# Spreading the weights' sums of an encoder block over mixer B, mixer A, the output branches and the output projection

## The chip, the cores and the metric

The kernel runs on one core of a Trainium2 chip. The core has five engines with a queue of their own each: TensorE (PE: matmuls and transposes), VectorE (DVE), ScalarE (ACT), GpSimd (POOL) and SyncE (SP). Each works off its queue in order. Here SP issues every DMA transfer. The metric is the device time of one execution in microseconds (us), lower is better.

## The reference, cut to what matters

One layer of a bidirectional encoder, for two sequences of 512 tokens with 1024 channels and shared weights, in float32:

```python
mod = silu(c) @ w_ada + b_ada                      # six vectors: sh1, sc1, gt1, sh2, sc2, gt2
h = rmsnorm(x, g_attn) * (1 + sc1) + sh1
z = h @ w_in                                       # mixer A, mixer B, two gates
oa = window_attention(...)                         # mixer A: 8 heads, 2 key heads, window of 128
ob = dense_attention(...)                          # mixer B: 8 heads, low-rank q and kv
mix = sigmoid(gla) * (oa @ w_o_a) + sigmoid(glb) * (ob @ w_o_b)    # the branches
x = x + gt1 * (mix @ w_out)                        # the output projection
h2 = rmsnorm(x, g_ffn) * (1 + sc2) + sh2
u = dwconv(h2 @ w_up, conv_w, conv_b)              # up-projection to 2 x 2816
ua, ug = split(u)
x = x + gt2 * ((silu(ug) * ua) @ w_down)
```

## The kernel before, in words

A product in float32 is made of three matmuls (`mm3`, L79): both operands are split into a high and a low part, and the product of the two low parts is left out. The splitting of weights is done by POOL (`split_pool`, L69) or by ACT and DVE (`split_fast`, L75).

The stages that matter here stand one after the other:

- **Mixers B and A** (L463 to L753). The rounds of one loop (L727) go over 64 units of mixer B and then 64 of mixer A. A unit is the scores of one head for 128 tokens. For each, PE makes scores (`scores`), DVE and ACT the softmax, POOL scales the rows by the inverse of their sum (L539), and PE transposes them (L545) three rounds later. Between, PE makes the matmuls of the two gates (`gates`, tile psg, L495); their results go out as gate_d.
- **Weights' sums** (`weight_sums`, L504). The up-projection below is computed from seven products of block sums in place of eight products of blocks (in the manner of Strassen and Winograd). Four of its weight operands are sums of four blocks of w_up. POOL makes them with four operations (L522 to L526) on a tile wsum that SP has loaded; SP then stores the tile to su_d in DRAM. There are 22 pieces c of w_up, each in two halves of 256 columns, so 44 tiles of 512 KB each, in two buffers. The generator is advanced by one step per round (L749), so one tile is done in three rounds. `keep_in_program_order` pins these instructions: POOL and SP keep the order in which they are written.
- **Branches** (L786 to L827). For each of 8 pieces f of 128 output channels, wo is loaded and split by POOL (`w_branch`), and for each sequence 24 matmuls follow (`branches`, tile psy); the gates come back as gt. At f = 4 the first half of w_out is loaded and split by POOL into the eight wt tiles (`w_half(0)`, L827).
- **Output projection** (L898 to L950). Two halves of 512 columns. `project_half` goes over two sequences and four blocks of tokens; each `project` is 24 matmuls (tile psx), a scaling and an addition on DVE, and a store to x1_d (L885). The second half's weights (`w_half(1)`, L949) take the same eight wt buffers, through seven raw buffers (wraw, L763), and are split by ACT and DVE.
- **Up-projection with convolution** (tiles px, py, pz, L980) and **down-projection** (psd). The first read of su_d is at 790.9 us.

PE's queue is fixed by the order in which the kernel is written, up to the choices of a scheduler; SP's and POOL's queues hold the pinned instructions in their written order, with the others between them.

Of the kernel before, what the change touches and what calls it, by code (L numbers as in the profile page):

```python
# [31 lines left out]
GW = 4 * AD + 2 * AD  # L32
FF = 2816
NP = FF // 128
EPS = 1e-6
BIG = -1e30

# [2 lines left out]
def encoder_block(ctx, tc, x, c_t, w_ada0, b_col, w_ada, b_ada, cols, w_z, w_g, gains, tabs, sink,  # L40
# [87 lines left out]
    with ExitStack() as st:  # L128
# [184 lines left out]
        with ExitStack() as s0:  # L313
# [140 lines left out]
            for _ in mods:  # L454
                pass

    mp = ctx.enter_context(tc.tile_pool(name="mp", bufs=1))

    def mblk(name, tag, shape=None, dt=F32R):
# [3 lines left out]
    with ExitStack() as st:  # L463
# [7 lines left out]
        def gates():  # L471
# [15 lines left out]
            for n in range(2 * KD):  # L487
                f, m = divmod(n, 2)
                for b in range(NB):
# [8 lines left out]
                    go = gw.tile([128, S], F32, name="go", bufs=2)  # L498
                    A.copy(go, ps)
                    SY.dma_start(gate_d[b, f, :, m], go)  # L500

        def weight_sums():  # L504

            pin = tc.keep_in_program_order
            halves = [(c, slice(256 * q, 256 * (q + 1))) for c in range(NP) for q in range(2)]
            ts = {}

            def load(n):  # L510
                if n < len(halves):
                    c, cs = halves[n]
                    ts[n] = gw.tile([128, 4, 256], F32, name="wsum", bufs=2)
                    pin(SY.dma_start(ts[n], w_up[c].rearrange("m q p n -> p (m q) n")[:, :, cs]))

            load(0)
            yield
            yield
            for n, (c, cs) in enumerate(halves):
                t = ts[n]  # L520
                load(n + 1)
                pin(G.tensor_add(t[:, 3], t[:, 2], t[:, 3]))  # L522
                pin(G.tensor_sub(t[:, 2], t[:, 0], t[:, 2]))
                yield
                pin(G.tensor_sub(t[:, 0], t[:, 3], t[:, 0]))
                pin(G.tensor_sub(t[:, 1], t[:, 1], t[:, 0]))  # L526
                yield
                pin(SY.dma_start(su_d[c, :, :, cs], t))
                yield

        def softmax(ps, n, plen):

# [179 lines left out]

        blocks = [PairB(b, g) for b in range(NB) for g in range(BH // 2)] + [GroupA(b, g) for b in range(NB) for g in range(AKV)]
        gate = gates()
        wsum = weight_sums()

        def fill(n):
            for _ in range(n):
# [8 lines left out]
        for n in range(len(todo) + LAG + 2):  # L727
            if n < len(todo):
                blk, u, first = todo[n]
                if first:  # L730
                    for _ in nxt:
                        pass
                    bi, since = blocks.index(blk), 0
                    nxt = blocks[bi + 1].prep() if bi + 1 < len(blocks) else iter(())
                scored.append((blk, u, blk.scores(u)))
            fill(5)
            for blk_, h in heads:
                blk_.values(h)
            heads = []
            if scored and (n >= LAG):  # L740
                blk_, u_, p_ = scored.pop(0)
                h = blk_.spread(u_, p_)
                if h is not None:
                    heads.append((blk_, h))
            if n < len(todo):
                if since >= blk.prep_from:
                    next(nxt, None)
                since += 1
            next(wsum, None)  # L749
        for _ in gate:  # L750
            pass
        for _ in wsum:
# [33 lines left out]
    with ExitStack() as s0:  # L786
        wk = s0.enter_context(tc.tile_pool(name="wko", bufs=2))
        ob = []
        raws = [mblk("o_raw0", "st", dt=F32), hblk("o_raw1", dt=F32)]
        for b in range(NB):  # L790
            SY.dma_start(raws[b], o_d[b].rearrange("q p n -> p q n"))
            o = [mblk(f"o{b}{q}", "st" if b else "pt") for q in range(2)]
            for q in range(8):
                split_fast(o[0][:, q, :], o[1][:, q, :], raws[b][:, q, :])
            ob.append(o)
        for b in range(NB):
            m_hi.append(hblk(f"m_hi{b}"))
            m_lo.append(hblk(f"m_lo{b}"))

        def w_branch(f):  # L800
            w = wk.tile([128, 2, 2, 4, 128], F32R, name="wo")
            for m in range(2):
                raw = wk.tile([128, 4, 128], F32, name="wo_raw", bufs=3)
                SY.dma_start(raw, w_o[f, :, m])
                split_pool(w[:, 0, m], w[:, 1, m], raw)
            return w

        def branches(f, b, w):
            gt = wk.tile([128, 2, S], F32, name="gt", bufs=2)
            SY.dma_start(gt, gate_d[b, f])  # L810
            A.activation(gt, gt, AF.Sigmoid)
            for m in range(2):
                ps = bank("psy")
                for k in range(4):
                    mm3(ps, w[:, 0, m, k, :], w[:, 1, m, k, :], ob[b][0][:, 4 * m + k, :], ob[b][1][:, 4 * m + k, :],
                        k == 0, k == 3)
                V.tensor_mul(gt[:, m, :], ps, gt[:, m, :])
            V.tensor_add(gt[:, 0, :], gt[:, 0, :], gt[:, 1, :])
            split_fast(m_hi[b][:, f, :], m_lo[b][:, f, :], gt[:, 0, :])

        for f in range(0, KD, 2):
            wo = [w_branch(f), w_branch(f + 1)]
            for b in range(NB):
                for q in range(2):
                    branches(f + q, b, wo[q])
            if f == 4:
                ws = w_half(0)  # L827

# [24 lines left out]
    with ExitStack() as s0:  # L853
# [91 lines left out]
            elif i == 2:  # L945
                first_sequence(0)

        project_half(0, (0, 1), lambda b, i: None)
        ws = w_half(1)  # L949
        project_half(1, (1, 0), operands)  # L950

# [217 lines left out]
```

## Time and profile before

| | |
|---|---|
| median of three runs | 1460.76 us (1458.72 to 1462.15) |
| profiled execution | 1463.69 us |
| its span in the trace | 1461.9 us |
| PE busy | 1395.4 us (95%) |
| DVE busy | 941.7 us (64%) |
| ACT busy | 679.5 us (46%) |
| POOL busy | 609.0 us (42%) |
| transfers | 255 MB, 175 GB/s on average |

A busy PE is not a PE at its peak: matmuls overlap, so a product of 512 columns is shown with 0.39 us where the next one starts 0.23 us later. What PE loses is read from the times at which it is not busy, from what ended them, and from the clock that was granted. In the trace, an idle time stands in brackets at the row of the instruction that came after it, with the instruction that released it.

### The profile page before, as it was taken

To read this page: it belongs to the slowest core of one execution; us is meant where nothing else is said; L and a number is where in the kernel's file an instruction comes from. 1 tells how busy PE (TensorE), PEld (TensorE's weight loads), DVE (VectorE), ACT (ScalarE), POOL (GpSimd) and SP (SyncE) were. 2 spreads that over 40 slices of the span, in tenths; PEclk is the share of its full clock that TensorE was granted. 3 is DMA by queue.
4 is the path that set the end of the run, shared out by engine and by line. 5 is a ranking of instruction groups with operands and counts; after the bars stand their busy time and mean duration, and the time that the engine had idled before them with its cause. 6 is when DMAs were issued, how large, how long until landed. Compare 5 with 4: busy or idle time off the path is not lost.

```text
span 1461.9 us, 21179 instructions
## 1 busy us (share of the span) xinstructions
PE 1395.4 (95%) x7184; PEld 1155.7 (79%) x7184; DVE 941.7 (64%) x1885; ACT 679.5 (46%) x1385; POOL 609.0 (42%) x702
## 2 busy tenths in 40 slices
PE   5888997999999899999998999999999999999998
PEld 4777776888878787787887888888888887888887
DVE  4788774666668786564369776666666668347433
ACT  3475223666666566332136765555555554212210
POOL 3175023676677787455003232222222235444430
PEclk9999999999999999999999999999999999999999
DMA  8565764666666667855432344444434447646522
GB/s 320 195 209 178 239 234 159 196 227 202 227 198 220 208 212 250 286 174 177 143 115 80 108 130 130 125 127 123 130 123 127 132 122 250 205 140 222 185 80 72
DMA packets 162620, 255.19 MB, mean 175 GB/s; under 512 B 21192, under 2 KB 86984, under 8 KB 159440
## 3 DMA queue, kind: packets, MB, share of 16 engines
q1 hardware_dynamic: 162512, 253.84, 53.2%
q8 instruction: 57, 0.93, 0.3%
q14 instruction: 51, 0.42, 0.1%
HBM read 186.67 MB, written 67.13 MB: 174 GB/s over the span
## 4 chain that ended last, share of the span: by engine, by line
PE 78%; DVE 10%; DMA 5%; POOL 3%; ACT 2%; issue 2%; SPq 0%; ACTq 0%; POOLq 0%; DVEq 0%
PE px L980 15%; PE psg L495 9%; PE py L980 8%; PE psd L80 5%; PE psd L81 5%; PE psd L82 5%; PE pz L980 4%; PE ppt L545 3%; PE ppo L608 2%; PE psx L82 2%; PE psx L81 2%; PE psx L80 2%; PE psz L80 1%; PE psz L82 1%; PE psz L81 1%
## 5 line engine op out<-in xcount | busy, mean ns | idle before, releaser
L959 POOL TENSOR_TENSOR wt<-wraw,wt 128x512 fp32r<-128x512 f32 x88 | 119.4, 1363 | 395.4 <-ACT wt L958 362.9
L980 PE MATMUL px<-t,wt 128*128 128x512 f32 x792 | 190.0, 389 | 1.7 <-ACT tmp_cc L985 1.7
L980 PEld LDWEIGHTS px<-t,wt 128*128 128x128 f32 x792 | 148.5, 188 | 33.1 <-ACT tmp_cc L985 2.4
L495 PE MATMUL psg<-h_hi,wg 128*128 128x512 f32 x512 | 172.1, 401 | 0.0
L77 DVE TENSOR_TENSOR wd<-wraw,wd 128x512 fp32r<-128x512 f32 x88 | 96.3, 1133 | 90.8 <-ACT wd L76 90.8
L80 PE MATMUL psd<-wd 128*128 128x512 f32 x352 | 137.0, 389 | 0.1
L82 PE MATMUL psd<-wd 128*128 128x512 f32 x352 | 136.9, 389 | 0.0
L81 PE MATMUL psd<-wd 128*128 128x512 f32 x352 | 136.9, 389 | 0.0
L76 ACT CAST wd<-wraw 128x512 fp32r<-128x512 f32 x88 | 50.8, 619 | 151.5 <-issue 112.7
L958 ACT CAST wt<-wraw 128x512 fp32r<-128x512 f32 x154 | 93.9, 619 | 39.7 <-POOL wt L959 26.5
L495 PEld LDWEIGHTS psg<-h_hi,wg 128*128 128x128 f32 x512 | 97.0, 192 | 18.7 <-POOL wg L73 0.8
L539 POOL TENSOR_SCALAR p<-p,l 128x512 f32<-128x512 f32 (+2 forms) x128 | 78.3, 615 | 63.7 <-DVE l L538 45.9
L495 PE MATMUL psg<-h_lo,wg 128*128 128x512 f32 x256 | 102.7, 401 | 0.0
L537 ACT ACTIVATE p<-pps,nm 128x512 f32<-128x512 f32 (+2 forms) x128 | 78.1, 610 | 39.2 <-DVE nm L534 31.3
L992 DVE SCALAR_TENSOR_TENSOR tmp_u<-tmp_cc,cw,tmp_u 128x511 f32<-128x511 f32 x66 | 57.2, 867 | 41.5 <-ACT tmp_u L991 41.4
L70 POOL TENSOR_SCALAR wd<-wraw 128x512 fp32r<-128x512 f32 x44 | 33.6, 764 | 112.5 <-PE psd L82 84.9
L80 PEld LDWEIGHTS psd<-wd 128*128 128x128 f32 x352 | 66.1, 188 | 14.3 <-issue 0.5
L82 PEld LDWEIGHTS psd<-wd 128*128 128x128 f32 x352 | 66.1, 188 | 13.8
L81 PEld LDWEIGHTS psd<-wd 128*128 128x128 f32 x352 | 66.1, 188 | 13.5
L534 DVE TENSOR_REDUCE nm<-pps 128x1 f32<-128x512 f32 (+2 forms) x128 | 74.7, 584 | 3.2 <-PE pps L82 1.5
L545 PE MATMUL ppt<-ident,p 128*128 128x128 f32 x416 | 66.9, 274 | 8.2 <-POOL p L539 8.2
L73 POOL TENSOR_TENSOR wd<-wraw,wd 128x512 fp32r<-128x512 f32 x44 | 73.1, 1661 | 3.7
(256 smaller groups left out, 3425.7 us busy)
## 6 DMA issues: line engine op xcount, KB each, us to landing
w_ada<-in_w_ada_dram SPq DMA_DIRECT2D x24, 1024.0 KB, 5.5
wsum<-in_w_up_dram SPq DMA_DIRECT2D x44, 512.0 KB, 3.9
su_d<-wsum SPq DMA_DIRECT2D x44, 512.0 KB, 3.6
wraw<-su_d SPq DMA_DIRECT2D x88, 256.0 KB, 3.1
wraw<-in_w_down_dram SPq DMA_DIRECT2D x88, 256.0 KB, 3.2
wraw<-in_w_up_dram SPq DMA_DIRECT2D x66, 256.0 KB, 2.7
g_d<-tmp_u SPq DMA_DIRECT2D x44, 256.0 KB, 2.4
wraw<-g_d SPq DMA_DIRECT2D x44, 256.0 KB, 3.5
```

The source lines that it names most:

```text
L77: V.tensor_sub(lo, raw, hi.bitcast(F32))
L80: PE.matmul(ps, lhsT=lh, rhs=rh, start=first, stop=False)
L81: PE.matmul(ps, lhsT=lh, rhs=rl, start=False, stop=False)
L82: PE.matmul(ps, lhsT=ll, rhs=rh, start=False, stop=last)
L495: PE.matmul(ps, lhsT=ws[n][:, wl, k, :], rhs=hl[b][:, k, :], start=k == 0 and i == 0, stop=k == KD - 1 and i == 2)
L534: V.tensor_reduce(nm, ps[:, :n], op=ALU.max, axis=AX.X, negate=True)
L537: A.activation(p[:, :n], ps[:, :n], AF.Exp, bias=nm, accum_out=l)
L539: G.tensor_scalar(out=p[:, :plen], in0=p[:, :plen], scalar1=l, scalar2=1.0, op0=ALU.mult, op1=ALU.mult)
L545: PE.transpose(pt[:, j * 128:(j + 1) * 128], p[:, j * 128:(j + 1) * 128], ident)
L958: A.copy(w[:, 0], raw)
L959: lo_eng.tensor_sub(w[:, 1], raw, w[:, 0].bitcast(F32))
L980: PE.matmul(ps[:, sl], lhsT=w[:, wl, i], rhs=h[:, hl, sl], start=not add and i == 0 and n == 0, stop=i == 3 and n == 2, skip_group_check=add)
```

## The change

The sums' generator moves out of the mixers and takes its tile, its width and its number as arguments. A list of 88 quarters of 128 columns is worked off in order by three users:

- in the mixers, 27 tiles of 256 columns in the same two buffers; it is advanced in each of the first 62 rounds, and in every third one after that;
- in the branches, 6 tiles of 256 columns in buffers of the wt pool, three steps behind each `branches`;
- in the projection's first half, 22 tiles of 128 columns in the tmp_cc buffers (six of them), nine steps behind each `project`.

In each, the load of the next tile is issued ahead of the sums of the present one, and the store behind them.

```diff
+    quarters = [(c, 128 * q) for c in ORDER for q in range(4)]
+
+    def weight_sums(tile, width, count):
+
+        pin = tc.keep_in_program_order
+
+        def load(n):
+            if n < count and quarters:
+                c, c0 = quarters[0]
+                del quarters[:width // 128]
+                t, cs = tile(), slice(c0, c0 + width)
+                pin(SY.dma_start(t, w_up[c].rearrange("m q p n -> p (m q) n")[:, :, cs]))
+                return t, su_d[c, :, :, cs]
+
+        nxt, n = load(0), 0
+        yield
+        yield
+        while nxt:
+            n += 1
+            (t, dst), nxt = nxt, load(n)
+            pin(G.tensor_add(t[:, 3], t[:, 2], t[:, 3]))
+            pin(G.tensor_sub(t[:, 2], t[:, 0], t[:, 2]))
+            yield
+            pin(G.tensor_sub(t[:, 0], t[:, 3], t[:, 0]))
+            pin(G.tensor_sub(t[:, 1], t[:, 1], t[:, 0]))
+            yield
+            pin(SY.dma_start(dst, t))
+            yield
...
-        wsum = weight_sums()
+        wsum = weight_sums(lambda: gw.tile([128, 4, 256], F32, name="wsum", bufs=2), 256, 27)
...
-            next(wsum, None)
+            if n < 62 or n % 3 == 2:
+                next(wsum, None)
...
+        wsum = weight_sums(lambda: wp.tile([128, 4, 256], F32, name="wsum", tag="wt", bufs=8), 256, 6)
         for f in range(0, KD, 2):
             wo = [w_branch(f), w_branch(f + 1)]
             for b in range(NB):
                 for q in range(2):
                     branches(f + q, b, wo[q])
+                    for _ in range(3):
+                        next(wsum, None)
...
-        project_half(0, (0, 1), lambda b, i: None)
+        wsum = weight_sums(lambda: tmp("cc").rearrange("p (m n) -> p m n", m=4), 128, 4 * NP)
+
+        def sums(b, i):
+            for _ in range(9):
+                next(wsum, None)
+
+        project_half(0, (0, 1), sums)
+        for _ in wsum:
+            pass
         ws = w_half(1)
```

The removed generator is the same with two halves per piece and a fixed tile. PE's queue holds the same instructions in the same order. Three places show what moves on POOL and SP. (Lines are those of the file to which a list belongs.)

POOL in the last quarter of mixer A, from one split of a gate's weights (wg) on. Before:

```order
L539 TENSOR_SCALAR p<-p,l 128x384
L522 TENSOR_TENSOR wsum<-wsum 128x256
L523 TENSOR_TENSOR wsum<-wsum 128x256
L539 TENSOR_SCALAR p<-p,l 128x256
L525 TENSOR_TENSOR wsum<-wsum 128x256
L526 TENSOR_TENSOR wsum<-wsum 128x256
L539 TENSOR_SCALAR p<-p,l 128x256
L539 TENSOR_SCALAR p<-p,l 128x384
L522 TENSOR_TENSOR wsum<-wsum 128x256
L523 TENSOR_TENSOR wsum<-wsum 128x256
```

And now:

```order
L480 TENSOR_TENSOR wsum<-wsum 128x256
L481 TENSOR_TENSOR wsum<-wsum 128x256
L542 TENSOR_SCALAR p<-p,l 128x256
L542 TENSOR_SCALAR p<-p,l 128x384 x2
L542 TENSOR_SCALAR p<-p,l 128x256 x2
L542 TENSOR_SCALAR p<-p,l 128x384 x2
L542 TENSOR_SCALAR p<-p,l 128x256 x2
L483 TENSOR_TENSOR wsum<-wsum 128x256
L484 TENSOR_TENSOR wsum<-wsum 128x256
```

Where two scalings of rows (p) stood between a tile's sums, nine do now.

SP at the end of the projection's first half, around the last load of w_out, which is the eighth wt tile of the second half. Before (x1_1 is a block of x1 that is stored, wraw a raw piece of a weight):

```order
L885 DMA x1_d_65<-x1_0_8006 128x512
L885 DMA x1_d_65<-x1_1_8007 128x512 x3
L764 DMA wraw_8304<-in_w_out_dram 128x512
L764 DMA wraw_8820<-in_w_up_dram 128x512
L764 DMA wraw_8825<-in_w_up_dram 128x512
```

And now (tmp_cc holds a quarter's sums):

```order
L892 DMA x1_d_65<-x1_1_7930 128x512
L486 DMA su_d_67<-tmp_cc_8182 512x1x128
L471 DMA tmp_cc_8196<-in_w_up_dram 128x4x128
L486 DMA su_d_67<-tmp_cc_8189 512x1x128
L471 DMA tmp_cc_8235<-in_w_up_dram 128x4x128
L768 DMA wraw_8381<-in_w_out_dram 128x512
L768 DMA wraw_8897<-in_w_up_dram 128x512
L486 DMA su_d_67<-tmp_cc_8196 512x1x128
```

The load of w_out stands behind 15 stores and 17 loads of quarters now, counted from the first x1 store on.

POOL at the change from mixer A to the branches, where the last scaling of mixer A (p, L539) and the first split of a branch's weights (wo) stand. Before:

```order
L539 TENSOR_SCALAR p_7128<-p_7128,l_7129 128x256
L526 TENSOR_TENSOR wsum_7000<-wsum_7000 128x256
L522 TENSOR_TENSOR wsum_7093<-wsum_7093 128x256
L523 TENSOR_TENSOR wsum_7093<-wsum_7093 128x256
L525 TENSOR_TENSOR wsum_7093<-wsum_7093 128x256
L526 TENSOR_TENSOR wsum_7093<-wsum_7093 128x256
L522 TENSOR_TENSOR wsum_7173<-wsum_7173 128x256
L523 TENSOR_TENSOR wsum_7173<-wsum_7173 128x256
L525 TENSOR_TENSOR wsum_7173<-wsum_7173 128x256
L526 TENSOR_TENSOR wsum_7173<-wsum_7173 128x256
L70 TENSOR_SCALAR wo_7346<-wo_raw_7347 128x512
L73 TENSOR_TENSOR wo_7346<-wo_raw_7347,wo_7346 128x512
```

And now:

```order
L542 TENSOR_SCALAR p_7022<-p_7022,l_7023 128x256
L71 TENSOR_SCALAR wo_7227<-wo_raw_7228 128x512
L74 TENSOR_TENSOR wo_7227<-wo_raw_7228,wo_7227 128x512
L71 TENSOR_SCALAR wo_7227<-wo_raw_7232 128x512
L74 TENSOR_TENSOR wo_7227<-wo_raw_7232,wo_7227 128x512
L71 TENSOR_SCALAR wo_7236<-wo_raw_7237 128x512
L74 TENSOR_TENSOR wo_7236<-wo_raw_7237,wo_7236 128x512
L71 TENSOR_SCALAR wo_7236<-wo_raw_7241 128x512
L74 TENSOR_TENSOR wo_7236<-wo_raw_7241,wo_7236 128x512
L480 TENSOR_TENSOR wsum_7279<-wsum_7279 128x256
```

The nine sums behind the last scaling are gone, and the first sum of the branches stands behind the eight operations of four splits. From it on, twelve sums stand in a row, then a split of the next wo, two sums, a split of another, and ten sums more.

## Rows read from the trace of the kernel before

**Rows 1.** The page's 40 slices of the span, busy tenths of PE and POOL.
```profile
PE   5888997999999899999998999999999999999998
POOL 3175023676677787455003232222222235444430
```

**Rows 2.** Waits, 445 to 600 us: waiter, waited for, total us, times, longest.
```profile
POOL wsum L522 <- DMA wsum<-in_w_up_dram: 22.6, 10, 4.8
PE ppt L545 <- POOL p L539: 8.2, 5, 3.4
```

**Rows 3.** Timeline of PE in mixer A: start, us, instruction, idle before and releaser.
```profile
497.76 0.44 PE L545 MATMUL ppt<-ident,p 128*128 128x128 f32 x2 [3.36 <-POOL p L539]
...
583.65 0.44 PE L545 MATMUL ppt<-ident,p 128*128 128x128 f32 x2 [3.34 <-POOL p L539]
```

**Rows 4.** Timeline of POOL ahead of the first of these two waits.
```profile
489.33 0.73 POOL L525 TENSOR_TENSOR wsum<-wsum 128x256 f32<-128x256 f32 x1
490.14 0.74 POOL L526 TENSOR_TENSOR wsum<-wsum 128x256 f32<-128x256 f32 x1
495.73 0.72 POOL L522 TENSOR_TENSOR wsum<-wsum 128x256 f32<-128x256 f32 x1 [4.84 <-DMA wsum<-in_w_up_dram]
...
497.23 1.60 POOL L539 TENSOR_SCALAR p<-p,l 128x256 f32<-128x256 f32 x3
```

**Rows 5.** Timeline of SP's issues at the same place.
```profile
489.66 0.38 SPq L514 DMA_DIRECT2D wsum<-in_w_up_dram  x1
490.91 0.52 SPq L528 DMA_DIRECT2D su_d<-wsum  x1
491.48 0.63 SPq L500 DMA_DIRECT2D gate_d<-go  x1
```

**Rows 6.** Windows behind both waits: length, busy us, granted clock, DMA share, GB/s.
```profile
498.00:503.00 5.00, 5.00 (x21) 4.19 (x20) 2.83 (x9) 1.38 (x4) 2.73 (x5) 0.66 0.97 351
583.00:589.00 6.00, 5.35 (x21) 4.66 (x22) 1.39 (x3) 2.06 (x5) 4.17 (x7) 0.72 0.36 115
```

**Rows 7.** Timeline of PE, the first idle times of the branches.
```profile
600.56 0.47 PE L80 MATMUL psy<-o,wo 128*128 128x512 f32 x1 [0.77 <-POOL wo L73]
...
609.82 0.50 PE L80 MATMUL psy<-o,wo 128*128 128x512 f32 x1 [0.82 <-POOL wo L70]
...
611.49 0.50 PE L82 MATMUL psy<-o,wo 128*128 128x512 f32 x1 [0.93 <-POOL wo L73]
```

**Rows 8.** Timeline of POOL, the split that ended the second of them.
```profile
608.79 0.98 POOL L70 TENSOR_SCALAR wo<-wo_raw 128x512 fp32r<-128x512 f32 x1 [6.55 <-DMA wo_raw<-in_w_o_dram]
```

**Rows 9.** Window of the projection's first half: PE, PEld, DVE, ACT, POOL, clock, DMA.
```profile
705.00:738.00 33.00, 33.00 (x147) 27.36 (x146) 13.46 (x22) 9.56 (x22) 0.00 (x0) 1.00 0.33 109
```

**Rows 10.** DMA issues by kind: count, KB each, median us from issue to landing.
```profile
wsum<-in_w_up_dram SPq DMA_DIRECT2D x44, 512.0 KB, 3.9
...
wraw<-su_d SPq DMA_DIRECT2D x88, 256.0 KB, 3.1
...
wraw<-in_w_up_dram SPq DMA_DIRECT2D x66, 256.0 KB, 2.7
...
x_d<-x SPq DMA_DIRECT2D x8, 256.0 KB, 2.0
```

**Rows 11.** POOL's groups by shape: count, busy us, mean ns, idle before.
```profile
L523 POOL TENSOR_TENSOR wsum<-wsum 128x256 f32<-128x256 f32 x44 | 33.0, 751 | 3.2
...
L327 POOL TENSOR_TENSOR t2b<-qf,tsb 128x128 f32<-128x128 f32 x8 | 3.8, 481 | 0.0
```

**Rows 12.** Timeline of SP: first x1 store, and the eighth tile's load.
```profile
705.80 0.33 SPq L885 DMA_DIRECT2D x_d<-x  x1
...
733.78 0.33 SPq L764 DMA_DIRECT2D wraw<-in_w_out_dram  x1
```

**Rows 13.** Timeline of ACT: casts of the second half's weight tiles.
```profile
734.23 3.55 ACT L76 CAST wt<-wraw 128x512 fp32r<-128x512 f32 x6
```

**Rows 14.** Timeline of PE: a product on the second half's eighth tile.
```profile
741.72 0.39 PE L80 MATMUL psx<-wt,m_hi 128*128 128x512 f32 x1
```

More of the change, by code (lines that the diff above doesn't have):

```diff
@@ L34 @@
 NP = FF // 128
+ORDER = range(NP)
 EPS = 1e-6
@@ L500, in gates @@
                     SY.dma_start(gate_d[b, f, :, m], go)
[L504 to L529, printed above, removed]
         def softmax(ps, n, plen):
```

## The prediction

> **What bounds the kernel now.** I read the 40 slices first. TensorE (PE) is busy in nearly every slice [rows 1], and the chain that ended last runs over it; so a change elsewhere is worth only the time for which PE waits. GpSimd (POOL) is full in the middle of the span and has empty slices right behind [rows 1], which is where this change goes: the sums of the up-projection's weights (the wsum tiles) are done beside the attention blocks, and the work after them leaves POOL idle.
>
> Second, the waits of the mixer A stretch, 445 to 600 us. PE waited 8.2 us, five times, on the scaling of the softmax rows (L539) that POOL does; POOL itself waited 22.6 us on loads of wsum [rows 2]. Two of PE's five waits, 3.36 and 3.34 us, hold most of it [rows 3]. Third, the timeline shows how one comes about: POOL's queue is in order, its first sum (L522) waits 4.84 us for a load, and three scalings that stand behind it run only after it [rows 4]. The load came late because SP issued it at 489.66 and it landed 6 us later [rows 4, 5]; with two buffers, a load can go out only when the store of two halves earlier is done.
>
> Fourth, the granted clock. After each of the two long waits PE ran at the lower level, 1.2 GHz, for a while: means of 0.66 over 5 us and 0.72 over 6 us [rows 6]. That is 5 x 0.34 = 1.7 and 6 x 0.28 = 1.7 us of lost matmul time, besides the waits.
>
> **Part 1, fewer sums in mixer A: a gain.** Mixer B keeps its 20 halves of 256 columns. Mixer A has 7 where it had 24, one step of the generator in three rounds instead of in each. Each load goes out some nine rounds before its sum, so the waits of rows 2 on wsum should end, and with them PE's. Removed: 8.2 us of waiting and 2 x 1.7 us of low clock, 11.6 us. PE has no other idle time between 445 and 585 us than these waits, and no row shows DVE or ACT ending one there, so I take it whole. The lower end is 8 us (the short waits stay, clock half regained).
>
> **Part 2, six halves in the branches.** POOL now splits the first branch weights (wo) right behind the last scaling; before, nine sums stood ahead of them. But PE's first branch product waits for the last gate product to be copied out by ACT, so the 0.77 us there [rows 7] stays, whoever the row names. The fourth wo_raw load was late: POOL waited 6.55 us for it and PE 0.82 and 0.93 us [rows 7, 8]. It stood behind a 512 KB store of sums that is now gone from there; I take 1.0 of the 1.75 us as gained. Against it, 24 sums stand between later wo splits, with loads of 3.9 us [rows 10]. Each block of four takes 4 x 0.81 = 3.2 us (the spacing in rows 4), and the order places a block with its load where PE still has one or two branch calls of 24 products in hand. I count nothing for these and keep 4 us for the range.
>
> **Part 3, 22 quarters in the output projection's first half: a loss.** POOL did nothing at all in this stretch [rows 9], and 88 sums of 128 columns there would cost nothing. What costs is **SP's queue**. Every quarter has a load and a store, pinned in order on SP: load 1, load 2, store 1, load 3, store 2, load 4 and so on. A store waits for its sums, and whatever stands behind it on SP waits too. So at most two quarters are under way at a time, though six buffers are there. And behind the 15th store and the 17th load stands a load that PE needs: the eighth and last weight tile of the projection's second half (wraw from w_out), which before went out at 733.78 [rows 12].
>
> The period of the loop: from the end of a quarter's sums, 0.03 us to the store's issue and 0.57 to the next issue (490.14 + 0.74 = 490.88 to 490.91, then 491.48) [rows 4, 5]; the load's landing, L; 0.1 to POOL's start (an estimate); four sums. A POOL operation of 128x128 took 0.48 us, one of 128x256 0.75 [rows 11], and two sums in a row leave 0.07 between them [rows 4], so four take 4 x 0.55 = 2.2 us. Two quarters therefore take 2.9 + L. L isn't in the trace (256 KB in pieces of 512 bytes): loads of 256 KB took 2.7 and 3.1 us, the sums' own 512 KB 3.9, and the quickest transfer of 256 KB, a store, 2.0 [rows 10]. I take 3.1, because it reads from and writes to the same places at that size, and keep 2.0 and 3.9 as ends.
>
> The first load stands behind the first x1 store, which went out at 705.80 [rows 12]: issue at 706.2, first quarter done at 706.2 + 3.1 + 0.1 + 2.2 = 711.6. The 15th is done seven pairs later, 711.6 + 7 x 6.0 = 753.6. Then store, load and our load: 1.1 us of issue, 3.1 of landing, and 0.6 for the cast by ACT that gives the high half [rows 13]: 758.4. PE wants this tile at 741.72, the first of the last three products of the second half's first projection [rows 14]. **PE waits 758.4 - 741.7 = 16.7 us.** After it the clock is low again, 1.7 us as in rows 6: together 18.4 us. The x1 stores and the last quarters then lag on SP as well, until about 775 us, but the tiles they free are wanted later than that once PE itself is late; I count nothing.
>
> **The sum**: -11.6 - 1.0 + 18.4 = +5.8 us. The profiled execution took 1463.69 us for a span of 1461.9, 2.9 above the median of 1460.76. The difference is put on the median: 1460.8 + 5.8 = **1466.5 us**, 0.4% slower. With L = 2.0 the 15th quarter ends at 710.5 + 7 x 4.9 = 744.8, PE goes on at 748.5, waits 6.8 + 1.7, and the sum is -4.1: 1456.7. With L = 3.9: 712.4 + 7 x 6.8 = 760.0, PE goes on at 765.6, waits 23.9 + 1.7, and the sum is +13: 1473.8.
>
> **Rivals.** *The projection keeps up* (faster): if the quarters ran as fast as they are handed out, three to each projection of 24 products, the eighth tile would be there in time and only the gains stay: 1460.8 - 12.6 = 1448. Against it stands that the two in flight would have to take (741.7 - 4.8 - 711.6) / 7 = 3.6 us a pair, less than a landing and four sums together. For it only that POOL and the DMA engines have room (DMA share 0.33) [rows 9].
>
> *The loads are quick* (no change). A transfer with little beside it might land at the lowest row of a load of this size, 2.7 us [rows 10]. A pair then takes 5.6, the 15th quarter ends at 711.2 + 39.2 = 750.4, PE goes on at 754.8, and the sum is -12.6 + 13.1 + 1.7 = +2.2: 1463. For it speaks that the DMA engines are a third busy there [rows 9], against it that the loads that take 2.7 come in larger pieces. The Trainium skill (DMA: Bandwidth & Descriptors, "Anatomy of one DMA") gives about 2.0 us fixed plus the bytes over 436 GB/s, for another issuing path than this one; for 256 KB that is an estimate of 2.6 us, and the sum by it would be about +1.5. The trace has 2.7 and 3.1 for loads of that size [rows 10], so it agrees in kind, and the rows are a little slower.
>
> *The branches stall too* (slower still). POOL's queue is in order there as well: if a sum ahead of a wo split waits for its load as L522 did, the split comes up to 3.9 us late [rows 10], and PE waits for it. At two of the three places where sums stand ahead of a split, less the slack, some 6 us on top: 1472. It decides when a load goes out later than about 4 us before POOL reaches it; SP's order has stores and gate loads ahead of these loads, which speaks for it.
>
> **How the numbers follow.** Forecast 0.58, keeping up 0.12, quicker loads 0.17, stalls in the branches too 0.13. About 0.2% (2.9 us) is what a measurement of this kernel tells from no change: below 1457.9 is faster, above 1463.7 slower. Of the forecast's chance 0.05 lies below that (L near 2.0) and 0.05 within it. Faster: 0.12 + 0.05 = 0.17. Same: 0.15 of the quicker loads and 0.05 make 0.20. Slower: 0.48 + 0.13 + 0.02 = 0.63. Range: 1455 to 1477, which leaves out the first rival and a little above the ends of L.
>
> **What would show it.** Right: in mixer A no wait of PE on POOL's scaling, and no wait of POOL on wsum loads; in the second half's first projection one wait of PE of 12 to 24 us before its last three products, ended by ACT's cast of the eighth tile, with the load of it issued near 755; sums on POOL up to about 775 at some 3 us a quarter; a low clock after the wait. Wrong: if the load goes out before 740, the queue argument fails, and the kernel is faster. If PE still waits on POOL in mixer A, part 1 fails. If the wait is there but short, only L was off.

## The result, and the profile after

The changed kernel takes 1479.1 us (median of four runs, 1474.07 to 1484.62) against 1460.5 us before: a ratio of 1.0128, with a 95% interval of 1.0087 to 1.0169. That is 18.6 us more, where 5.8 were forecast. The profiled execution is the slowest of the four, 1484.62 us with a span of 1482.8, so the accounts below add up to 1482.8 - 1461.9 = 20.9 us.

PE's queue holds the same instructions in the same order as before, so the two timelines can be laid side by side. These are the rows of PE's timeline after the change that answer to [rows 3], [rows 7] and [rows 14] (start, us, instruction, in brackets the idle time before it and its releaser). Here and below only the rows that a reading rests on are shown; others may lie between them.

```profile
586.40 0.47 PE L81 MATMUL psy<-o,wo 128*128 128x512 f32 x1 [0.77 <-POOL wo L74]
...
610.66 0.50 PE L83 MATMUL psy<-o,wo 128*128 128x512 f32 x1 [1.08 <-POOL wo L74]
617.05 0.50 PE L81 MATMUL psy<-o,wo 128*128 128x512 f32 x1 [1.10 <-POOL wo L71]
618.90 0.62 PE L83 MATMUL psy<-o,wo 128*128 128x512 f32 x1 [1.12 <-POOL wo L74]
...
663.87 0.79 PE L81 MATMUL psy<-o,wo 128*128 128x512 f32 x1 [4.42 <-POOL wo L71]
...
756.01 0.80 PE L81 MATMUL psx<-wt,m_hi 128*128 128x512 f32 x1 [18.27 <-ACT wt L77]
784.48 1.64 PE L873 MATMUL pst<-ident,x 128*128 128x128 f32 x13 [2.23 <-DVE x L899]
819.36 2.13 PE L873 MATMUL pst<-ident,x 128*128 128x128 f32 x11 [2.40 <-DVE x L899]
```

Three differences of start times give the balance:

| stretch | before | after | difference |
|---|---|---|---|
| start to the first product of the branches | 600.56 | 586.40 | -14.2 |
| from there to the point at which PE wants the eighth w_out tile | 141.2 | 151.3 | +10.2 |
| the wait for that tile | 0 | 18.3 | +18.3 |
| from that product to the end | | | +6.6 |

**The mixers** gained, and mixer A as forecast. The waits of PE on the row scaling are gone but for one of 0.16 us. PE's last products of mixer B start at 439.90 before and at 437.62 after:

```profile
439.90 1.79 PE L608 MATMUL ppo<-p,vsb 128*128 128x512 f32 x7
```

```profile
437.62 1.91 PE L611 MATMUL ppo<-p,vsb 128*128 128x512 f32 x7 [0.53 <-DVE p L551]
```

From there to the first product of the branches it is 160.66 us before and 148.78 after, so 11.9 of the 14.2 us lie behind mixer B. The other 2.3 lie ahead of this point, which the changed kernel and its variants reach anywhere from 431.6 to 438.0 us.

**The branches** lost. Besides the wait of 0.77 us at their first product, which is the same in both, PE waits there seven times for POOL's splits of wo, 9.2 us in all, where five waits made 4.3 us before. The clock, at 1.00 in this stretch before, was low behind two of the places (windows of the kernel after: length, busy us of PE, PEld, DVE, ACT and POOL, granted clock, DMA share, GB/s):

```profile
619.00:624.00 5.00, 5.00 (x15) 3.98 (x16) 2.88 (x5) 1.80 (x3) 4.76 (x6) 0.66 0.36 142
664.00:670.00 6.00, 5.40 (x12) 3.81 (x13) 2.88 (x3) 1.06 (x2) 5.73 (x7) 0.50 0.50 178
```

That is 5.0 x 0.34 + 5.4 x 0.50 = 4.4 us of lost matmul time. With the 4.9 us of waits it makes 9.3 of the 10.2 us.

**The projection** has the forecast wait, 18.27 us on the eighth tile. Its cause stands in SP's timeline, in the rows that answer to [rows 12]:

```profile
750.70 0.52 SPq L486 DMA_DIRECT2D su_d<-tmp_cc  x1
751.26 0.63 SPq L471 DMA_DIRECT2D tmp_cc<-in_w_up_dram  x1
751.94 0.56 SPq L768 DMA_DIRECT2D wraw<-in_w_out_dram  x1
```

The load that PE waits for (L768) goes out at 751.94, directly behind a store and a load of quarters. Each store goes out when its four sums are done. POOL's timeline shows the pace, at the first sum of each quarter:

```profile
742.65 0.45 POOL L480 TENSOR_TENSOR tmp_cc<-tmp_cc 128x128 f32<-128x128 f32 x1 [0.53 <-DMA tmp_cc<-in_w_up_dram]
745.84 0.45 POOL L480 TENSOR_TENSOR tmp_cc<-tmp_cc 128x128 f32<-128x128 f32 x1 [1.15 <-DMA tmp_cc<-in_w_up_dram]
748.63 0.45 POOL L480 TENSOR_TENSOR tmp_cc<-tmp_cc 128x128 f32<-128x128 f32 x1 [0.74 <-DMA tmp_cc<-in_w_up_dram]
```

Two quarters take 748.63 - 742.65 = 5.98 us, and POOL waits for a load ahead of each. The windows view shows what the wait did to the clock:

```profile
745.00:756.00 11.00, 0.00 (x0) 0.00 (x0) 0.01 (x1) 0.62 (x1) 6.71 (x15) 0.50 0.79 239
756.00:762.00 6.00, 5.99 (x13) 4.46 (x14) 2.60 (x6) 2.21 (x4) 3.53 (x7) 0.50 0.78 231
762.00:765.00 3.00, 3.00 (x14) 2.44 (x13) 2.05 (x7) 0.00 (x0) 1.38 (x3) 0.92 0.69 194
```

PE stood still until 756.0, and then ran 6 us at 0.50 of full speed, which is 1.2 GHz, and 3 us at 0.92: 6 x 0.50 + 3 x 0.08 = 3.2 us. The remaining 3.4 us of the last stretch are the size of the waits on x at 784.48 (2.23, new) and 819.36 (2.40, before 1.21). Ahead of the first of them ACT had waited 6.29 us for an x1 store. These stores were late on SP: the block that was ready at 773.0 was stored at 776.17, behind the last quarter's store (774.43):

```profile
781.59 0.63 ACT L893 ACTIVATE tmp_u<-tmp_u 128x512 f32<-128x512 f32 x1 [6.29 <-DMA x_d<-tmp_u]
```

The second isn't put down to SP: it is 2.4 us in e6_mix38 as well, where the quarters end in time.

### The profile page after: what moved, and what is told of

Its sections match the earlier page's. It is cut to its first block, busy times and chain, and to the rows that moved or that the text cites. A ratio compares the mean times of both kernels' runs of the same rounds, so it can differ in the third digit from the quotient of the medians.

```text
span 1482.8 us, 21261 instructions
## 1 busy us (share of the span) xinstructions
PE 1401.8 (95%) x7184; PEld 1160.1 (78%) x7184; DVE 950.5 (64%) x1885; ACT 680.1 (46%) x1385; POOL 624.4 (42%) x746
## 4 chain that ended last, share of the span: by engine, by line
PE 71%; DVE 10%; DMA 8%; POOL 5%; ACT 3%; issue 2%; SPq 1%; ACTq 0%; DVEq 0%; POOLq 0%
PE px L995 15%; PE psg L527 10%; PE py L995 8%; PE psd L81 5%; PE psd L82 5%; PE psd L83 5%; PE pz L995 4%; PE ppt L548 3%; DMA tmp_cc<-in_w_up_dram 2%; PE ppo L611 2%; PE psz L81 1%; PE psz L83 1%; PE psz L82 1%; PE ppo L706 1%; PE pps L682 1%
## 5 line engine op out<-in xcount | busy, mean ns | idle before, releaser
L1006 ACT ACTIVATE tmp_u<-tmp_cc,cw 128x512 f32<-128x512 f32 x66 | 53.6, 812 | 36.2 <-DMA g_d<-tmp_u 25.8
```

## The experiments

Ratios are to the kernel before, run on the same chip. The profiled executions of the changed kernel and its variants start mixer B's last products anywhere from 431.6 to 438.0 us, so within the traces distances are compared and not absolute times. From there to the first product of the branches they all take 148.4 to 149.7 us, against 160.66 before: the gain in mixer A is there in each of them.

| kernel | median, us | ratio (95%) |
|---|---|---|
| the change | 1479.1 | 1.0128 (1.0087 to 1.0169) |
| e1_raw8 | 1483.8 | 1.0139 (1.0125 to 1.0152) |
| e2_mix33 | 1476.7 | 1.0096 (1.0079 to 1.0113) |
| e4_depth3 | 1476.1 | 1.0094 (1.0080 to 1.0108) |
| e7_poolq | 1473.5 | 1.0090 (1.0073 to 1.0106) |
| e9_branchq | 1486.1 | 1.0163 (1.0134 to 1.0193) |
| e5_all | 1465.6 | 1.0007 (0.9991 to 1.0023) |
| e10_numbers | 1461.3 | 0.9983 (0.9967 to 1.0000) |
| e11_raw8 | 1457.3 | 0.9958 (0.9935 to 0.9981) |
| e12_ahead | 1448.4 | 0.9879 (0.9853 to 0.9905) |
| e6_mix38 | 1444.3 | 0.9890 (0.9874 to 0.9907) |
| e8_mix38g | 1444.4 | 0.9894 (0.9875 to 0.9913) |

### e1_raw8: the eighth tile's load taken out of the queue's way

```diff
-        r = wp.tile([128, 512], F32, name="wraw", bufs=7)
+        r = wp.tile([128, 512], F32, name="wraw", bufs=8)
```

> One raw weight buffer more (eight wraw in place of seven), so that SP issues the load of the second half's eighth w_out tile before the projection, ahead of all quarters; nothing else is changed. Theory A (the 18.3 us wait is the late load alone): the wait and the low clock behind it (3.2 us) go, 1479.1 - 21.5 = about 1457.6. Theory B (SP's queue as a whole is late): the quarters' stores still end near 774, and the x1 stores of the second half stand behind them, each holding one of two tmp_u1 buffers; so the chain store, multiplication, store reaches the fourth block of the second sequence as late as before, near 783, and PE waits there, at the first transposes (pst), for about as long: 1474 to 1478. Theory C (the DMA engines are too full, not the queue): the early load changes nothing before the wait, and PE still waits on the eighth tile for over 10 us.

The wait on the eighth tile is gone, and the time is the same as that of the change (1.0139 against 1.0128, intervals that overlap). The waits stand elsewhere now, in PE's timeline:

```profile
770.31 0.47 PE L873 MATMUL pst<-ident,x 128*128 128x128 f32 x1 [14.82 <-DVE x L899]
775.85 0.47 PE L873 MATMUL pst<-ident,x 128*128 128x128 f32 x1 [5.07 <-DVE x L899]
782.39 3.03 PE L873 MATMUL pst<-ident,x 128*128 128x128 f32 x13 [6.07 <-DVE x L899]
```

That is 26 us. ACT's waits in the same stretch (waiter, waited for, total us, times, longest) say why DVE was late:

```profile
ACT tmp_u L893 <- DMA x_d<-tmp_u: 39.4, 3, 30.0
```

ACT squares each block of x1 into a tmp_u1 buffer, and such a buffer comes free when the x1 store of an earlier block is done; that store stands on SP behind the quarters. So theory B holds, and more strongly than it said (1483.8 us lies above its 1474 to 1478): the load was only the first of several transfers that hung in this queue. Theory A falls, and so does C, since PE no longer waits for the tile.

### e7_poolq: the quarters' transfers off SP's queue

```diff
-                pin(SY.dma_start(t, w_up[c].rearrange("m q p n -> p (m q) n")[:, :, cs]))
+                pin(dma.dma_start(t, w_up[c].rearrange("m q p n -> p (m q) n")[:, :, cs]))
...
-            pin(SY.dma_start(dst, t))
+            pin(dma.dma_start(dst, t))
...
-        wsum = weight_sums(lambda: tmp("cc").rearrange("p (m n) -> p m n", m=4), 128, 4 * NP)
+        wsum = weight_sums(lambda: tmp("cc").rearrange("p (m n) -> p m n", m=4), 128, 4 * NP, dma=G)
```

> The changed kernel with one edit: in the projection, POOL issues the loads and stores of the 22 quarters itself, on its own queue, in place of SP. Mixers and branches are unchanged. Theory A (SP's queue, in which waiting stores stand ahead of PE's loads): SP's issues are back where they were in the kernel before, the eighth w_out tile is loaded as soon as a raw buffer is free, and PE's wait of 18.3 us, the later ones of 2.2 and 1.2 us and their low clock (5 us) go: about 1454 to 1458, what is left being the mixers' gain of 14 and the branches' loss of 10. Theory B (the DMA engines or the buffers, not the queue): the wait on the eighth tile or on the transposes stays above 10 us, 1470 or more. If POOL's issue costs several us each, the last sums end after 790 and the up-projection's first read of su_d waits: then a wait on wt from su_d appears behind 790, which neither theory counts.

SP's timeline shows the load of the eighth tile back at an early place, and PE doesn't wait for it:

```profile
723.39 0.33 SPq L768 DMA_DIRECT2D wraw<-in_w_out_dram  x1
```

So for the tile theory A holds: SP's order held the load back, and not the DMA engines. But the time, 1473.5 us, is that of theory B, because the buffers took over, at the transposes. POOL pays for the issues itself, as a quarter in its timeline shows:

```profile
741.28 0.51 POOL L480 TENSOR_TENSOR tmp_cc<-tmp_cc 128x128 f32<-128x128 f32 x1
...
743.83 0.73 POOL L486 DMA_DIRECT2D su_d<-tmp_cc  x1 [0.29 <-POOL tmp_cc L484]
744.51 0.79 POOL L471 DMA_DIRECT2D tmp_cc<-in_w_up_dram  x1
745.29 0.51 POOL L480 TENSOR_TENSOR tmp_cc<-tmp_cc 128x128 f32<-128x128 f32 x1
```

A quarter takes 4.0 us (741.28 to 745.29), and the last one is stored at 785. The quarters lie in the tmp_cc buffers, which DVE needs for its differences of x1. DVE's timeline and PE's behind it:

```profile
767.33 0.69 DVE L920 TENSOR_TENSOR tmp_cc<-e 128x512 f32<-128x512 f32 x1 [12.27 <-DMA su_d<-tmp_cc]
```

```profile
772.08 0.45 PE L873 MATMUL pst<-ident,x 128*128 128x128 f32 x1 [4.20 <-DVE x L899]
780.81 3.20 PE L873 MATMUL pst<-ident,x 128*128 128x128 f32 x13 [8.28 <-DVE x L899]
```

DVE waits 12.27 us for a quarter's store to free its buffer, the scaling of x (L899) stands behind that on DVE, and PE's transposes wait for it. The six buffers that the prediction counted were free only as long as the quarters ended in time.

### e4_depth3: what sets the quarters' pace

```diff
-        nxt, n = load(0), 0
+        queue, n = [load(i) for i in range(ahead)], ahead - 1
...
-            (t, dst), nxt = nxt, load(n)
+            queue.append(load(n))
+            t, dst = queue.pop(0)
...
-        wsum = weight_sums(lambda: tmp("cc").rearrange("p (m n) -> p m n", m=4), 128, 4 * NP)
+        wsum = weight_sums(lambda: tmp("cc").rearrange("p (m n) -> p m n", m=4), 128, 4 * NP, 3)
```

> In the projection, quarters are loaded three ahead in place of one (four of the six buffers are under way); mixers and branches are unchanged. In SP's queue the load of the eighth w_out tile now stands behind all 22 quarters, no longer behind 15. Theory A (two in flight set the pace of 3.0 us a quarter): the pace becomes POOL's own, about 2.2 us; 22 quarters from 704 end near 752, the eighth tile's load goes out near 752, so PE's wait stays at 17 to 20 us, but the x1 stores behind are on time and the later waits of 2.2 and 1.2 us with their low clock go: 1472 to 1476. Theory B (the DMA engines set the pace): it stays at 2.9 us, the quarters end near 768, PE waits about 35 us: 1490 or more.

POOL's timeline, the first sum of the first and of the twenty-first of the 22 quarters:

```profile
699.12 0.46 POOL L481 TENSOR_TENSOR tmp_cc<-tmp_cc 128x128 f32<-128x128 f32 x1 [32.40 <-DMA tmp_cc<-in_w_up_dram]
...
744.14 0.45 POOL L481 TENSOR_TENSOR tmp_cc<-tmp_cc 128x128 f32<-128x128 f32 x1
```

These are 20 quarters in 45.0 us, 2.25 us each. The change needed (771.91 - 703.92) / 21 = 3.24. So theory A holds: with one quarter loaded ahead, POOL waits for the loads, and with three the pace is its own. In SP's queue the eighth tile's load stands behind all 22 now:

```profile
746.21 2.52 SPq L487 DMA_DIRECT2D su_d<-tmp_cc  x2
748.82 0.58 SPq L769 DMA_DIRECT2D wraw<-in_w_out_dram  x1
```

PE's wait for it is 15.2 us, somewhat less than expected, and the wait at the first transposes is 0.2. The time, 1476.1, is within the expected range.

### e2_mix33 and e9_branchq: the branches

In e2_mix33 the six tiles of the branches go to the mixers:

```diff
-        wsum = weight_sums(lambda: gw.tile([128, 4, 256], F32, name="wsum", bufs=2), 256, 27)
+        wsum = weight_sums(lambda: gw.tile([128, 4, 256], F32, name="wsum", bufs=2), 256, 33)
...
-            if n < 62 or n % 3 == 2:
+            if n < 62 or n % 5 < 3:
```

> The six tiles of the branches go back to the mixers, which make 33 of 256 columns, the seven or so more in mixer A at three steps in five rounds; no sums in the branches; the projection's quarters are unchanged. Theory A (the branches lose 10 us because SP's stores of sums hold up the loads of wo, and POOL's sums its splits): PE's waits on wo splits in the branches fall from 9.2 us to 4.3 or less and the low clock there goes, and mixer A stays without waits: 1479.1 - 10 = about 1469. Theory B (PE comes to the branches 14 us earlier and meets wo loads that are late anyway): the waits there stay at 7 us or more, 1476 to 1479. Theory C (the mixers can't take 33): PE waits on the row scaling in mixer A again, 3 us or more, 1472 to 1476.

PE's timeline has two waits on wo left, of 2.00 and 0.62 us, and a longer one behind them:

```profile
653.98 0.78 PE L81 MATMUL psy<-o,wo 128*128 128x512 f32 x1 [2.00 <-POOL wo L71]
...
750.74 0.80 PE L81 MATMUL psx<-wt,m_hi 128*128 128x512 f32 x1 [22.71 <-ACT wt L77]
```

Of its mechanism, theory A is right: without sums there, the 9.2 us become 2.6, the stretch from the first product of the branches (586.37) to the point at which PE wants the eighth tile (750.74 - 22.71) is 141.7 us, as it was before the change, and mixer A takes 13 tiles with no wait of PE. Its time is wrong. The quarters don't hurry because PE comes earlier, so a good part of what the branches gave back was spent at the next wait: 22.7 us instead of 18.3. Of the 10 us, the ratios show some 5 (1.0096 against 1.0128, with intervals that overlap, so even this gain isn't shown).

In e9_branchq, POOL issues the branches' transfers of sums itself, as in e7_poolq:

```diff
-        wsum = weight_sums(lambda: wp.tile([128, 4, 256], F32, name="wsum", tag="wt", bufs=8), 256, 6)
+        wsum = weight_sums(lambda: wp.tile([128, 4, 256], F32, name="wsum", tag="wt", bufs=8), 256, 6, G)
```

> The changed kernel with one edit: in the branches, POOL issues the loads and stores of the six tiles itself, in place of SP. Theory A (in the branches, the loads of wo stand on SP behind stores that wait for sums): PE's waits on wo splits there, 9.2 us in seven places, fall to 4.5 or less. Theory B (the sums themselves, 24 at some 0.85 us on POOL, stand ahead of the splits): they stay at 7 us or more. In both cases the time hardly moves, 1473 to 1480: whatever PE gains here it waits longer for the eighth w_out tile, whose load hangs on the quarters' pace and not on PE.

The waits on wo didn't fall, five of them made 10.8 us, the first 4.65:

```profile
610.61 0.80 PE L81 MATMUL psy<-o,wo 128*128 128x512 f32 x1 [4.65 <-POOL wo L71]
```

This speaks for theory B, POOL's side, but it doesn't settle it. POOL also issued twelve transfers at 0.73 to 0.80 us, some 9 us, and its first sum, ahead of the split that PE waited for, itself waited 5.33 us for a load that POOL had only just issued. So one burden was taken from SP and another put on POOL. The time, 1486.1, lies above the expected range; the ratio's interval overlaps that of the change. How the branches' loss divides between POOL's sums and SP's stores stays open; e2_mix33 shows that the two together are the cause.

### e5_all, e6_mix38 and e8_mix38g: towards a version without the waits

e5_all joins the edits of e1, e2 and e4 and hands out the first quarters ahead of the first projection:

```diff
+        sums(0, 0)
         project_half(0, (0, 1), sums)
```

> All of it together: 33 tiles in the mixers, none in the branches, eight raw weight buffers, quarters loaded three ahead, and the first three quarters handed out ahead of the first projection, so that the loads go out some 30 us earlier. Theory A (each loss is a matter of SP's queue and of how early the loads go out): quarters end near 720, PE waits neither on the eighth tile nor on x1, the gain of the mixers stays: 1460.5 - 14 = about 1446.5, with 1449 as the upper end. Theory B (POOL or the DMA engines are too full for sums beside the branches' end and the projection): waits on wo or wt splits of 5 us or more come back, 1452 to 1460.

It ran at 1465.6 us, as fast as the kernel before. PE waits neither on wo for long nor on the eighth tile, but four times on x, 15.3 us. SP's and DVE's timelines name the transfer that was caught this time:

```profile
740.01 2.55 SPq L487 DMA_DIRECT2D su_d<-tmp_cc  x2
742.62 0.62 SPq L906 DMA_DIRECT2D tmp_u<-gt_d  x1
```

```profile
746.80 0.69 DVE L887 TENSOR_TENSOR tmp_u<-psx,tmp_u 128x512 f32<-128x512 f32 x1 [19.88 <-DMA tmp_u<-gt_d]
```

The load of the second half's gate row (L906) stands behind the last quarters' stores, and DVE waits 19.88 us for it. So 22 quarters are too many for the time before the second half, even at 2.2 us each. Theory A, that earliness and depth are enough, falls; but what came back isn't the wait of theory B on wo or wt either.

e6_mix38 keeps all of e5_all and changes the numbers: 38 tiles in the mixers, 12 quarters in the projection.

```diff
-        wsum = weight_sums(lambda: gw.tile([128, 4, 256], F32, name="wsum", bufs=2), 256, 33)
+        wsum = weight_sums(lambda: gw.tile([128, 4, 256], F32, name="wsum", bufs=2), 256, 38)
...
-            if n < 62 or n % 5 < 3:
+            if n < 62 or n % 4 < 3:
...
-        wsum = weight_sums(lambda: tmp("cc").rearrange("p (m n) -> p m n", m=4), 128, 4 * NP, 3)
+        wsum = weight_sums(lambda: tmp("cc").rearrange("p (m n) -> p m n", m=4), 128, 12, 3)
```

> As e5_all, but with 38 tiles of 256 columns in the mixers (18 of them in mixer A, three steps in four rounds) and only 12 quarters in the projection, three of them handed out ahead of it. Theory A (whatever stands behind the quarters on SP's queue is late until the last quarter is stored; in e5_all the gt row of the second half, issued at 742.6, on which DVE waited 19.9 us): 12 quarters at 2.2 us from 690 end near 717, so the gt row and the x1 stores are on time, PE has no wait at the transposes, and the gain of the mixers stays: 1461.5 - 14 = 1447 to 1450. Theory B (38 tiles bring mixer A's waits back, as the 44 of the kernel before): PE waits 3 to 8 us on the row scaling there, 1452 to 1457.

1444.3 us, a ratio of 0.9890 (0.9874 to 0.9907): 1.1% faster than the kernel before and 2.4% faster than the change, a little below the expected range. PE has no wait between 435 and 580 us, and none between 660 and 760; the last quarter is stored at 706.65, and the gate row follows at 707.21:

```profile
706.65 0.51 SPq L487 DMA_DIRECT2D su_d<-tmp_cc  x1
707.21 0.62 SPq L906 DMA_DIRECT2D tmp_u<-gt_d  x1
```

Theory A holds, and 38 tiles fit into the mixers.

> As e6_mix38, with the 12 quarters' loads and stores on POOL's own queue. If SP's queue still costs something in e6_mix38, this is faster than it by that; if nothing is left there, the two are equal within 2 us (about 1447 to 1450).

With the same numbers and POOL's own queue, e8_mix38g takes 1444.4 us. Nothing that the runs can show is left in SP's queue.

### e10_numbers, e11_raw8 and e12_ahead: which of the edits of e6_mix38 were needed

e10_numbers is the change with the numbers of e6_mix38 alone (38, none, 12).

> The changed kernel with other numbers alone: 38 tiles in the mixers (three steps in four rounds of mixer A), none in the branches, 12 quarters in the projection; seven raw buffers, one quarter loaded ahead and the start behind the first projection as in the changed kernel. Theory A (the pace of 3.0 us and the place on SP do no harm once there are few enough): first quarter done near 691, the twelfth near 725, the eighth tile's load right behind the x1 store at about 725, PE's wait on it 0 to 5 us: 1446 to 1451. Theory B (the deeper loads, the early start and the raw buffer of e6_mix38 made most of its gain over the changed kernel): PE waits over 8 us on the eighth tile or on x1, 1455 or more.

1461.3 us, equal to the kernel before. SP issued the eighth tile's load behind all twelve quarters, and PE waited 10.58 us:

```profile
731.09 0.52 SPq L486 DMA_DIRECT2D su_d<-tmp_cc  x1
...
732.37 0.40 SPq L768 DMA_DIRECT2D wraw<-in_w_out_dram  x1
```

Theory B holds: even twelve quarters are too many at 3.2 us each with a start at 688. e11_raw8 adds the eighth raw buffer to it, e12_ahead the deeper loads and the early start.

> e10_numbers (38 tiles in the mixers, 12 quarters in the projection, one loaded ahead, at a late start) with eight raw weight buffers alone, so that the eighth w_out tile is loaded before the quarters. Theory A (in e10_numbers the late eighth tile is the whole difference to e6_mix38): PE's wait of 10.6 us and the low clock behind it go and nothing takes its place, since the last quarter is stored at about 731, before the second half's x1 stores: 1461.3 - 13 to 16 = 1445 to 1449. Theory B (as in e1_raw8, the wait moves to the x1 stores and comes back at the transposes): PE waits 5 us or more on x there, 1453 or more.

> e10_numbers with the other two parts of e6_mix38 alone: quarters loaded three ahead, and three of them handed out ahead of the first projection; seven raw buffers. Theory A (the twelve quarters are out of SP's queue before the eighth tile's raw buffer is free, so the queue holds nothing up): the last quarter is stored near 710, the eighth tile is loaded by 720, PE doesn't wait on it: 1444 to 1449. Theory B (the eighth tile's load needs the extra buffer): a wait of 5 us or more on the eighth tile, 1452 or more.

e11_raw8 comes to 1457.3 us. The wait on the tile is gone, and two waits on x of 4.1 and 4.2 us take its place, for the reason of e1_raw8; its ACT waits show the x1 store:

```profile
ACT tmp_u L890 <- DMA x_d<-tmp_u: 14.7, 1, 14.7
```

e12_ahead comes to 1448.4 us, a ratio of 0.9879, which can't be told from e6_mix38 (0.9890). Its SP timeline has the last quarter out of the way before the tile's load:

```profile
712.23 0.51 SPq L487 DMA_DIRECT2D su_d<-tmp_cc  x1
718.51 0.57 SPq L769 DMA_DIRECT2D wraw<-in_w_out_dram  x1
```

So what is needed is that the quarters are through before anything that PE needs gets behind them. Whether the deeper loads or the early start would do alone was not run. Pulling out a single transfer, as the raw buffer does, gets a part of it at most (0.9958 against 0.9983 for e10_numbers, with intervals that overlap).

## Why the prediction was wrong in size

Slower was forecast, by one of the two mechanisms that were found, but with +5.8 us where the profiled spans differ by 20.9, and the median, 1479.1, lies above the range's end of 1477. The terms:

| term | forecast | measured |
|---|---|---|
| mixers | -11.6 | -14.2 (-11.9 behind mixer B) |
| branches | -1.0 | +10.2 |
| wait for the eighth tile | +16.7 | +18.3 |
| low clock behind it | +1.7 | +3.2 |
| later waits on x, 2.2 of it by x1 stores late on SP | 0 | +3.4 |
| sum | +5.8 | +20.9 |

**The step that failed is part 2**, the branches: 11 of the 15 us. Its small gain is there, the waits of 0.82 and 0.93 us on the fourth load are gone; its "I count nothing for these", for the 24 sums and their loads, is what failed. The prediction looked at each block of sums by itself, found that PE had products in hand there, and put the cost at nothing. But lateness on POOL's queue is carried on to the next place, and it comes out where PE has least in hand. That is at the last wo splits, behind the eight splits of w_half(0), where PE waited already before the change, in two rows that the prediction didn't weigh:

```profile
669.11 0.50 PE L80 MATMUL psy<-o,wo 128*128 128x512 f32 x1 [0.67 <-POOL wo L70]
671.35 0.50 PE L82 MATMUL psy<-o,wo 128*128 128x512 f32 x1 [1.52 <-POOL wo L73]
```

POOL had slack ahead of this place, but not enough. Its waits between the first product of the branches and these splits (waiter, waited for, total us, times, longest), before (600 to 669 us) and after (586 to 664):

```profile
POOL wo L70 <- PE psy L82: 22.7, 4, 11.5
POOL wo L70 <- DMA wo_raw<-in_w_o_dram: 6.5, 1, 6.5
```

```profile
POOL wo L71 <- DMA wo_raw<-in_w_o_dram: 12.9, 3, 5.7
POOL wsum L480 <- DMA wsum<-in_w_up_dram: 3.5, 3, 1.8
```

Before, POOL was ahead of PE and waited 22.7 us for it. The sums, some 21 us (24 at about 0.85), took up about that much by themselves. What came on top are the waits that their transfers brought: 3.5 us for wsum, and 6.4 more for wo. POOL's longest wait for wo behind the first block of sums, and SP's rows ahead of it:

```profile
638.36 0.62 POOL L71 TENSOR_SCALAR wo<-wo_raw 128x512 fp32r<-128x512 f32 x1 [4.65 <-DMA wo_raw<-in_w_o_dram]
```

```profile
631.78 0.52 SPq L486 DMA_DIRECT2D su_d<-wsum  x1
633.02 1.93 SPq L808 DMA_DIRECT2D wo_raw<-in_w_o_dram  x3
```

The loads of wo stood behind the store of the last tile of sums, as the eighth tile's load did later behind the quarters. The last splits came 8.9 us later behind the first product than before (663.20 - 586.40 against 668.43 - 600.56), and PE's wait there became 4.42 us, with others on the way. The third rival (1472, the branches stall too) named the place, but with two late loads of sums as its price; e2_mix33 ties the loss to the sums there and their transfers together.

**Part 1** was right in its mechanism: PE's waits on the scaling are gone, and POOL's on wsum loads with them. Its size was right too: 11.9 us behind mixer B where 11.6 were forecast. The other 2.3 us lie ahead of mixer B's last products and can't be told from the spread between executions.

**Part 3** was right in mechanism and near in size. The period of two quarters was forecast as 6.0 us and is 5.98 in POOL's rows above; a load issued at 742.71 let POOL start at 745.84, 3.1 us later, as taken. By the estimate of 2.6 us from the Trainium skill (DMA: Bandwidth & Descriptors, "Anatomy of one DMA"), whose fit is for another issuing path, this load would have come 0.5 us sooner; the measurement decides. That the load's issue, 751.94, lies so near to the forecast 754.7 is in part luck, since two deviations cancel: the first quarter's sums began at 703.92, since the first x1 store went out at 698.97 and not at 705.80, and some pairs took longer, so that the mean over all quarters is 3.24 us. PE wanted the tile 4 us earlier than forecast, at 737.7, and that makes the wait longer.

**The low clock** was taken from the 5 to 6 us behind waits of 3.4 us [rows 6]. Behind a wait of 18 us the clock was already at 0.50 during the wait and stayed there for 6 us, which cost 3.2 us in place of 1.7.

**"I count nothing" for the x1 stores** was wrong as well. In the change itself they cost 2.2 us of waiting. e1_raw8 shows what this step really hid: with the wait for the tile gone, they cost 26 us of waits, as much as that wait with what followed it. The prediction asked which transfer behind the quarters is needed first, and took the others to be covered; they were covered only by the first one's wait.

What the first rival described (1448, the projection keeps up) is reached by e6_mix38 and e12_ahead, at 1444 and 1448, but only with fewer quarters, none of the sums in the branches and earlier loads.

## What to carry to other kernels

An engine that is idle in a stretch is not yet a free place for work: the work brings transfers, and on a queue that issues in order a store that waits for its sums holds up every load behind it. List all that stands behind, not only what is needed first, since taking away the first wait uncovers the next (the tile, the x1 stores, the gate row, the buffers, one after the other here). And before work is put on an engine, look for a place further on where someone already waits for that engine, and for the slack ahead of it: what is added beyond that slack, the waits for the new transfers included, comes out there.

## What the runs showed of the hardware

- A DMA that POOL issues took mostly 0.73 to 0.80 us of POOL's own time, with 0.29 us of idle time before the store, so a quarter cost 4.0 us there against 2.25 with SP issuing (e7_poolq, e4_depth3).
- Behind PE's wait of 18 us the clock was granted at 0.50 for 6 us of full work and was back within the next 3; behind the wait of 4.42 us in the branches of the change it was at 0.50 for 6 us too, so the wait four times as long cost hardly more clock behind it; behind the waits of 3.4 us before the change it had averaged 0.66 over 5 us and 0.72 over 6 [rows 6].
- The 16 loads of wo took a median of 5.2 us from issue to landing in the change, with the sums' transfers among them on SP, against 3.1 before. Where these transfers were gone (e2_mix33) or issued by POOL (e9_branchq) it was 3.3.
